# Four modulation pieces, and the first two, as float32 products in two column groups

## The chip, the cores and the metric

The kernel runs on one core of a Trainium2 chip. The metric is the device time of one launch in microseconds (us), as the median of several runs. Traces come from one profiled execution.

## The reference

Two transformer blocks run behind each other on 512 latent rows of width 1024, the first of them with two layers and with 256 context rows beside the latent ones. Everything is float32. What the change touches is in the first block:

```python
for l in range(DEPTH):                      # DEPTH = 2
    last = l == DEPTH - 1
    mod = silu_c @ w_ada[l] + b_ada[l]      # w_ada[l]: 1024 x 6144, six pieces of 1024 columns
    sh1, sc1, gt1, sh2, sc2, gt2 = [m[:, None, :] for m in jnp.split(mod, 6, axis=-1)]
    modc = silu_cc @ w_ada[l] + b_ada[l]
    shc1, scc1, gtc1, shc2, scc2, gtc2 = jnp.split(modc, 6)
    hc = modulate(rmsnorm(xc, g_mix[l]), shc1, scc1)
    pc = hc @ (w_in[l][:, :KV_END] if last else w_in[l])
    ctx_kv = kv_heads(pc[..., :KV_END], kg_a[l], kg_b[l], None)
    h = modulate(rmsnorm(x, g_mix[l]), sh1, sc1)
    p = h @ w_in[l]
    x = x + gt1 * latent_mixer(p, ctx_kv, ...)
    h2 = modulate(rmsnorm(x, g_ffn[l]), sh2, sc2)
    x = x + gt2 * expert_choice_ffn(h2, w_router[l], w_e_gate[l], w_e_up[l], w_e_down[l])
    if not last:
        xc = xc + gtc1 * context_mixer(pc, ctx_kv, ...)
        hc2 = modulate(rmsnorm(xc, g_ffn[l]), shc2, scc2)
        xc = xc + gtc2 * expert_choice_ffn(hc2, w_router[l], w_e_gate[l], w_e_up[l], w_e_down[l])
```

A mixer projects, attends (two kinds of attention and a short convolution), gates the branches (`w_branch`) and ends in the product with `w_out`. The expert stage sends each of 16 experts its best rows by a router. The conditioning has only two rows, `silu_c` and `silu_cc`, so a modulation piece is a product of two rows with 1024 x 1024 weights (4 MB).

## The kernel before

**Order of the stages.** Loading and the first two modulation pieces (0 to about 60 us in the trace), latent mixer of layer 0 (to about 662), context mixer of layer 0 (to 917), experts of layer 0 over latent and context rows together (949 to 1530), latent mixer of layer 1 (to 2180), the last expert stage (`last_experts`, 2222 to about 2670), then the second block.

**Dense products.** Weights come in chunks of 512 KB through `weights`: SP issues the load into `raw` (L92), ScalarE rounds it to `wh` (L95), VectorE subtracts to `wl` (L96), and TensorE runs three matmuls of the reduced float32 format for each pair of operands (L82 to L84). The pools in `self.wps` take turns; `nraw` and `nw` are the number of `raw` buffers and of `wh` and `wl` buffers. The context mixer has two pools, one of 3 and 3 and one of 2 and 2 (`w1`). The expert stages load chunks of 1 MB as `eraw`; the one of layer 0 splits them (`eh` on ScalarE, `el` on VectorE), `last_experts` multiplies them as plain float32 (L1273).

**Modulation.** `ada(l, pieces)` is a generator that the mixers step in the background, one step each `period` ticks. A step is a quarter of a piece: two chunks by `weights`, 16 matmuls with `wh` (L441) and `wl` (L442), a copy on ScalarE, two transposes (L447). In layer l's latent mixer the pieces 2 to 5 of that layer run so, in the context mixer the pieces 0 and 1 of layer 1. The pieces 0 and 1 of layer 0 run ahead of everything in `first_ada`: 64 matmuls of 256 columns in plain float32 (L478) on 16 loads `wada` of 512 KB (L475). `first_gather` runs one small indirect load on GpSimd in the first mixer.

**The end of a mixer.** The product with `w_out` hands each of 8 feature rows to `residual`, which loads `xo` (L928, SP), forms `xn` (L929, VectorE), then `put` forms `u` on ScalarE and the router's matmuls (L970). `finish` sums the norm (L979), forms the affinities `aff`, runs top-k, and transposes `u` (`hpt`, L1002) into token rows `tok`, which GpSimd stores to `h2d` (L1015); the rows are gathered for the experts by an indirect load on GpSimd (L1140, in the last stage L1280) and transposed (`ept`, L1132).

**What sets the order.** The code is recorded and a scheduler orders the instructions of each engine ahead of time. An engine runs its list in order: a load on SP that waits for its buffer holds all the loads behind it.

## Time and profile before

| | us |
|---|---|
| median of 3 runs | 3576.55 (3576.17 to 3577.59) |
| the profiled execution | 3583.02 |
| its span in the trace | 3581.3 |
| TensorE busy | 3354.1 (94%) |
| TensorE weight loads | 2572.3 (72%) |
| VectorE busy | 2268.4 (63%) |
| ScalarE busy | 1732.4 (48%) |
| GpSimd busy | 274.4 (8%) |
| mean granted TensorE clock | 0.977 |

PE is TensorE's matmuls, DVE VectorE, ACT ScalarE, POOL GpSimd, SP the engine that issues most loads. Busy time is a union of instruction spans; a plain float32 matmul leaves two records. "PEclk" is the granted TensorE clock as a share of full speed. A chain of waits shows "[idle before <-releaser]" behind an instruction that its engine sat idle for.

### The profile page before, as it was taken

The numbers are of one execution on the slowest core, as the hardware profiler recorded it, in microseconds if no ns is written. First come the engines' busy times: TensorE is split into PE (matmuls) and PEld (weight loads), VectorE is DVE, ScalarE is ACT, GpSimd is POOL, SyncE is SP. The second block draws the span as 40 slices with busy tenths as digits, with TensorE's granted clock in tenths as the row PEclk, the third lists the DMA queues.
The fourth block names the chain that finished last, engine by engine and source line by source line (L and its number), as shares of the span: only waits on it lengthen the run. The fifth ranks groups of instructions, "written<-read, shape, count | busy, mean of one in ns | idle before, by whom it ended". The sixth has DMA issues, their size and how long they took to land. (4 is left out here: it accounts for less than half of the span.)

```text
span 3581.3 us, 46471 instructions
## 1 busy us (share of the span) xinstructions
PE 3354.1 (94%) x17762; PEld 2572.3 (72%) x17762; DVE 2268.4 (63%) x3543; ACT 1732.4 (48%) x2542; POOL 274.4 (8%) x322
## 2 busy tenths in 40 slices
PE   8999999999799999989999996998889999989998
PEld 5787777898688888877777774332228887768887
DVE  4787676588599999977776753232235456854444
ACT  3555554456477777745555542110115355633333
POOL 1101110000200000021011101000001000010000
PEclk9999999999899999989999997999999999999999
DMA  6332437458799999933334376999993432244332
GB/s 218 119 100 93 135 122 220 145 168 239 269 373 335 367 339 341 350 127 95 100 101 130 121 235 255 421 421 421 421 367 103 128 87 88 84 130 138 100 94 83
DMA packets 369227, 732.90 MB, mean 205 GB/s; under 512 B 25534, under 2 KB 262060, under 8 KB 342636
## 3 DMA queue, kind: packets, MB, share of 16 engines
q1 hardware_dynamic: 355728, 695.15, 55.1%
q0 software_dynamic: 7184, 33.31, 2.4%
q8 instruction: 140, 2.29, 0.3%
q10 hardware_dynamic: 6092, 1.47, 0.2%
q14 instruction: 83, 0.68, 0.1%
HBM read 683.71 MB, written 46.14 MB: 204 GB/s over the span
## 5 line engine op out<-in xcount | busy, mean ns | idle before, releaser
L96 DVE TENSOR_TENSOR wl<-raw,wh 128x1024 fp32r<-128x1024 f32 (+2 forms) x423 | 506.6, 1200 | 370.6 <-ACT wh L95 362.9
L95 ACT ACTIVATE wh<-raw 128x1024 fp32r<-128x1024 f32 (+2 forms) x423 | 436.6, 1034 | 490.4 <-PE d L83 301.0
L82 PE MATMUL d<-hh,wh 128*128 128x512 f32 (+1 forms) x1304 | 485.4, 373 | 5.5 <-ACT hh L301 4.3
L83 PE MATMUL d<-hl,wh 128*128 128x512 f32 (+1 forms) x1304 | 484.1, 371 | 1.8 <-DVE hl L302 1.6
L84 PE MATMUL d<-hh,wl 128*128 128x512 f32 (+1 forms) x1304 | 484.3, 372 | 0.4 <-DVE wl L96 0.4
L1116 DVE TENSOR_TENSOR el<-eraw,eh 128x2048 fp32r<-128x2048 f32 x192 | 433.8, 2287 | 33.2 <-ACT eh L1115 32.5
L1115 ACT ACTIVATE eh<-eraw 128x2048 fp32r<-128x2048 f32 x192 | 365.3, 1918 | 105.6 <-PE pup L84 39.3
L82 PEld LDWEIGHTS d<-hh,wh 128*128 128x128 f32 x1304 | 247.6, 190 | 44.1 <-ACT hh L301 5.1
L83 PEld LDWEIGHTS d<-hl,wh 128*128 128x128 f32 x1304 | 247.3, 190 | 39.8 <-DVE hl L302 4.6
L84 PEld LDWEIGHTS d<-hh,wl 128*128 128x128 f32 x1304 | 247.3, 190 | 39.2 <-DVE wl L96 2.3
L642 ACT ACTIVATE prob<-S,st 128x768 f32<-128x768 f32 (+3 forms) x176 | 134.5, 764 | 142.2 <-DVE st L640 66.9
L1332 DVE SCALAR_TENSOR_TENSOR y<-pdn,route,y 64x512 fp32r<-64x512 f32 x32 | 24.0, 750 | 280.6 <-ACT y L1331 280.5
L82 PE MATMUL d<-wh,hh 128*128 128x256 f32 (+1 forms) x528 | 161.2, 305 | 1.9 <-ACT hh L301 1.8
L83 PE MATMUL d<-wl,hh 128*128 128x256 f32 (+1 forms) x528 | 159.9, 303 | 0.3 <-DVE wl L96 0.3
L84 PE MATMUL d<-wh,hl 128*128 128x256 f32 (+1 forms) x528 | 159.7, 303 | 0.2 <-DVE hl L302 0.2
L638 DVE TENSOR_REDUCE st<-S 128x1 f32<-128x768 f32 (+3 forms) x176 | 137.2, 783 | 23.5 <-PE S L703 21.3
L658 ACT ACTIVATE pth<-ppt 128x512 fp32r<-128x512 f32 x184 | 106.0, 595 | 74.8 <-PE ppt L655 71.5
L659 DVE TENSOR_TENSOR ptl<-ppt,pth 128x512 fp32r<-128x512 f32 x184 | 122.6, 685 | 27.2 <-ACT pth L658 26.1
L1273 PE MATMUL pdn<-eraw,at 128*64 128x512 f32 x512 | 119.0, 599 | 21.1 <-DMA eraw<-in_w_e_down 16.4
L655 PE MATMUL ppt<-ident,prob 128*128 128x128 f32 x736 | 121.6, 277 | 7.2 <-DVE prob L647 6.6
L1273 PE MATMUL pup<-eraw,xt 128*64 128x512 f32 x512 | 119.9, 600 | 6.0 <-DMA eraw<-in_w_e_up 6.0
L1273 PE MATMUL pga<-eraw,xt 128*64 128x512 f32 x512 | 118.5, 605 | 2.7 <-DMA eraw<-in_w_e_gate 2.7
(546 smaller groups left out, 7596.4 us busy)
## 6 DMA issues: line engine op xcount, KB each, us to landing
eraw<-in_w_e_gate SPq DMA_DIRECT2D x128, 1024.0 KB
eraw<-in_w_e_up SPq DMA_DIRECT2D x128, 1024.0 KB
eraw<-in_w_e_down SPq DMA_DIRECT2D x128, 1024.0 KB
raw<-in_w_in SPq DMA_DIRECT2D x170, 512.0 KB
raw<-in_w_ada SPq DMA_DIRECT2D x80, 512.0 KB
raw<-in_w_ff SPq DMA_DIRECT2D x64, 512.0 KB
raw<-in_w_out SPq DMA_DIRECT2D x32, 512.0 KB
raw<-in_w_branch SPq DMA_DIRECT2D x48, 256.0 KB
```

Of the source, the lines that this page charges most:

```text
L82: mm(ps, wh, xh, start=first, stop=False, skip_group_check=skip)
L83: mm(ps, wh, xl, start=False, stop=False, skip_group_check=skip)
L84: mm(ps, wl, xh, start=False, stop=last, skip_group_check=skip)
L95: for ins in (nc.scalar.activation(h[:, :n], raw[:, :n], AF.Copy), nc.vector.tensor_sub(l[:, :n], raw[:, :n], h[:, :n])):
L96: nc.vector.tensor_sub(l[:, :n], raw[:, :n], h[:, :n])):
L638: nc.vector.tensor_reduce(nm, S[:, s0:s1], axis=AX, op=ALU.max, negate=True)
L642: nc.scalar.activation(p, S[:, s0:s1], AF.Exp, bias=nm, accum_out=ls)
L655: nc.tensor.transpose(pt[:, h * 128:h * 128 + 128], probs[h], self.ident)
L659: nc.vector.tensor_sub(pl, pt, ph)
L1115: nc.scalar.activation(h, raw, AF.Copy)
L1116: nc.vector.tensor_sub(lo, raw, h)
L1273: nc.tensor.matmul(ps[halves[j], :], x(k), raw[:, i, j * 512:j * 512 + 512], start=k == 0, stop=k == 7, skip_group_check=True)
```

## The change

Six edits, all in the first block:

1. `ada_between` (new) forms a piece as plain float32 products without splits: for each of 8 slices of 128 rows two matmuls of 512 columns, one into PSUM partitions 0 and 1, one into 64 and 65 (two column groups), then two copies on ScalarE, eight transposes, and `modulation` (new). The mixer calls `between()` behind the `w_out` product and ahead of `finish()`. In the context mixer it forms (0, 5), (1, 0) and (1, 1), the pairs being (layer, piece), with 24 chunk loads `zraw` of 512 KB in 5 buffers of a new pool `z`; in layer 1's latent mixer it forms (1, 5) with four `zraw` of 1 MB in the two `qT` buffers of attention. These four leave the background.
2. `first_ada` runs the pieces 1 and 0 side by side in the two column groups, on the same loads.
3. The context mixer's second weight pool goes: 3 `raw` and 3 `w` buffers in place of 5 and 5.
4. The background in the latent mixers has three pieces and a period of 4 in place of four and 3.
5. `finish` takes its small sum from pool `pd` (now called `nps`) in place of an attention bank.
6. `first_gather` goes; the context residual's store goes from GpSimd's queue to ScalarE's.

```diff
     def first_ada(self, raw):
...
         for q in range(4):
-            for p in (1, 0):
-                ps = self.pd.tile([128, 512], F32, name="d", tag="d")[:2, :256]
-                c0 = p * 1024 + q * 256
-                for ch in range(0, 8, 4):
+            ps = self.pd.tile([128, 512], F32, name="d", tag="d")[:, :256]
+            for ch in range(0, 8, 4):
+                ws = []
+                for p in (1, 0):
                     w = raw[:, n % 4].rearrange("p (k f) -> p k f", k=4)
                     n += 1
+                    c0 = p * 1024 + q * 256
...
-                    for k in range(4):
-                        nc.tensor.matmul(ps, self.cs[:, ch + k, :], w[:, k], start=ch + k == 0, stop=ch + k == 7)
+                    ws.append(w)
+                for k in range(4):
+                    for h, w in zip((0, 64), ws):
+                        nc.tensor.matmul(ps[h:h + 2], self.cs[:, ch + k, :], w[:, k], start=ch + k == 0,
+                                         stop=ch + k == 7, skip_group_check=True)
...
-    def first_gather(self):
...
+    def ada_between(self, l, p, raw, banks, row):
...
+        nc = self.nc
+        ps, pt = banks()
+        k = 0
+        while k < 8:
+            w = raw()
+            n = w.shape[1]
+            nc.sync.dma_start(w, self.A["w_ada"][l][k * 128:(k + n) * 128, p * 1024:p * 1024 + 1024]
+                              .rearrange("(i p) f -> p i f", p=128))
+            for i in range(n):
                 for j in range(2):
+                    nc.tensor.matmul(ps[64 * j:64 * j + 2], self.cs[:, k, :], w[:, i, j * 512:j * 512 + 512],
+                                     start=k == 0, stop=k == 7, skip_group_check=True)
+                k += 1
+        for j in range(2):
+            rows = row()
+            nc.scalar.activation(rows[:2], ps[64 * j:64 * j + 2], AF.Copy)
+            for m in range(4):
+                n = (j * 4 + m) * 2
+                nc.tensor.transpose(pt[:, n:n + 2], rows[:2, m * 128:m * 128 + 128], self.ident[:2, :2])
+        self.modulation(l, p, pt[:, :16], 0, 8)
...
         self.do(self.fm(self.A["w_out"][l], 8, 0, 1024, mh, ml, T, residual))
+        between()
         finish()
...
         def finish():
-            if lat:
-                ps = self.ps.tile([128, 1024], F32, name="S", tag="S")
-            else:
-                ps = self.ps.tile([128, 512], F32, name="S", tag="Sc", bufs=2)
+            ps = self.pd.tile([128, 512], F32, name="nps", tag="d")
...
-                    self.background, self.ticks, self.period = [self.ada(l, (2, 3, 4, 5))], -6, 3
-                    if first:
-                        self.background.append(self.first_gather())
...
+                    self.background, self.ticks, self.period = [self.ada(l, (2, 3, 4))], -6, 4
+
+                    def between():
+                        if first:
+                            return
+                        S = self.ps.tile([128, 1024], F32, name="S", tag="S")
+                        self.ada_between(l, 5, lambda: self.ap.tile([128, 4, TL], F32R, name="zraw", tag="qT", bufs=2)
+                                         .rearrange("p (i a) t -> p i (a t)", i=2).bitcast(F32),
+                                         lambda: [S[:, :512], S[:, 512:]],
+                                         lambda: self.pp.tile([128, 512], F32R, name="zrow", tag="pth").bitcast(F32))
...
-                        more = self.pool(e1, "w1"), 2, 2
+                        zp = self.pool(e1, "z", 5, side="right")
                         self.open_dense(e1, nraw=3, nw=3, side="right")
-                        self.wps.append(more)
+
+                        def between():
+                            for m, p in ((0, 5), (1, 0), (1, 1)):
+                                self.ada_between(m, p, lambda: zp.tile([128, 1, 1024], F32, name="zraw", tag="zraw"),
+                                                 lambda: [self.ps.tile([128, 512], F32, name="S", tag="Sc", bufs=2)
+                                                          for _ in range(2)],
+                                                 lambda: zp.tile([128, 512], F32, name="zrow", tag="zrow", bufs=2))
...
-                        self.background = [self.top_k(True, fp), vectors(), self.load_vectors_2(), self.ada(1, (0, 1))]
+                        self.background = [self.top_k(True, fp), vectors(), self.load_vectors_2()]
...
-                        nc.gpsimd.dma_start(xCd, xC)
+                        nc.scalar.dma_start(xCd, xC)
```

The lists of instructions show three places where the order moves. Buffer numbers stand behind the names; lines of the changed kernel lie 25 to 27 further down (L1002 is L1027 there, L970 is L998, L928 is L955, L1269 is L1294), and L518 is the float32 product of a piece.

TensorE at the end of layer 0's latent mixer, before: `hpt` are the transposes of its `finish`, `d_6501` is the first product of the context mixer.

```order
L84 MATMUL d_6266<-mh_5774,wl_6300 128x512
L1002 MATMUL hpt_6370<-ident_117,u_5975 128x128 x4
L1002 MATMUL hpt_6376<-ident_117,u_5975 128x128 x3
L82 MATMUL d_6501<-wh_6491,hh_6482 128x256
L83 MATMUL d_6501<-wl_6492,hh_6482 128x256
L84 MATMUL d_6501<-wh_6491,hl_6483 128x256
```

And in the changed kernel, where that first product is `d_6340`:

```order
L998 MATMUL o_5853<-wr_5815,u_5814 128x16 x4
L1004 MATMUL nps_6188<-ones_125,acc_5852 128x1 x4
L1027 MATMUL hpt_6215<-ident_117,u_5814 128x128
L1027 MATMUL hpt_6223<-ident_117,u_5814 128x128 x4
L1027 MATMUL hpt_6229<-ident_117,u_5814 128x128 x4
L1027 MATMUL hpt_6237<-ident_117,u_5814 128x128 x4
L1027 MATMUL hpt_6243<-ident_117,u_5814 128x128 x4
L1027 MATMUL hpt_6251<-ident_117,u_5814 128x128 x4
L1027 MATMUL hpt_6257<-ident_117,u_5814 128x128 x4
L82 MATMUL d_6340<-wh_6330,hh_6321 128x256
L83 MATMUL d_6340<-wl_6331,hh_6321 128x256
```

The context mixer's first product, which stood behind seven of the 32 transposes, now stands behind all of them.

TensorE at the end of the context mixer, before, from the last matmuls of `w_out` (`d_9782`) on; `o` is the router's sum, `S` the norm's:

```order
L83 MATMUL d_9782<-ml_9225,wh_9815 128x256
L84 MATMUL d_9782<-mh_9224,wl_9816 128x256
L1002 MATMUL hpt_9913<-ident_117,u_9503 128x128 x4
L1002 MATMUL hpt_9920<-ident_117,u_9503 128x128 x2
L970 MATMUL o_9542<-wr_9504,u_9503 128x16 x2
L1002 MATMUL hpt_9920<-ident_117,u_9503 128x128
L970 MATMUL o_9542<-wr_9504,u_9503 128x16 x2
L979 MATMUL S_9861<-ones_125,acc_9541 128x1 x2
L1002 MATMUL hpt_9920<-ident_117,u_9503 128x128
```

And in the changed kernel, where the last `w_out` product is `d_9327` and the norm's sum `nps_9549` comes six rows behind the last one shown:

```order
L84 MATMUL d_9327<-mh_8847,wl_9361 128x256
L518 MATMUL S_9406<-zraw_9424,cs_147 2x512 x2
L518 MATMUL S_9406<-zraw_9428,cs_147 2x512
L998 MATMUL o_9087<-wr_9049,u_9048 128x16 x2
L518 MATMUL S_9406<-zraw_9428,cs_147 2x512
L518 MATMUL S_9406<-zraw_9432,cs_147 2x512 x2
L518 MATMUL S_9406<-zraw_9436,cs_147 2x512 x2
L1027 MATMUL hpt_9601<-ident_117,u_9048 128x128 x4
L1027 MATMUL hpt_9608<-ident_117,u_9048 128x128 x2
L526 MATMUL S_9407<-ident_117,zrow_9440 128x2 x4
L526 MATMUL S_9407<-ident_117,zrow_9446 128x2 x4
L518 MATMUL S_9453<-zraw_9455,cs_147 2x512 x2
```

The float32 products of the pieces stand between the last `w_out` matmul and the last router matmuls.

SP at the end of layer 1's latent mixer, before: `raw` are chunks of `w_out`, `xo` residual loads, `eraw` the chunks of the last expert stage.

```order
L1269 DMA eraw_20812<-in_w_e_up 128x2048
L928 DMA xo_20385<-xLd_67 128x512
L92 DMA raw_20505<-in_w_out 128x4x256
L1269 DMA eraw_20818<-in_w_e_up 128x2048
L92 DMA raw_20535<-in_w_out 128x4x256
L928 DMA xo_20408<-xLd_67 128x512
L1269 DMA eraw_20824<-in_w_e_up 128x2048
L1269 DMA eraw_20830<-in_w_e_up 128x2048
L928 DMA xo_20469<-xLd_67 128x512
L928 DMA xo_20492<-xLd_67 128x512
L928 DMA xo_20553<-xLd_67 128x512
L928 DMA xo_20576<-xLd_67 128x512
```

And in the changed kernel:

```order
L955 DMA xo_20012<-xLd_67 128x512
L955 DMA xo_20035<-xLd_67 128x512
L955 DMA xo_20096<-xLd_67 128x512
L955 DMA xo_20119<-xLd_67 128x512
L514 DMA zraw_20143<-in_w_ada 128x2x1024
L514 DMA zraw_20149<-in_w_ada 128x2x1024
L1294 DMA eraw_20419<-in_w_e_gate 128x2048
L1294 DMA eraw_20366<-in_w_e_gate 128x2048
L1294 DMA eraw_20372<-in_w_e_gate 128x2048
L1294 DMA eraw_20378<-in_w_e_gate 128x2048
L1294 DMA eraw_20384<-in_w_e_gate 128x2048
```

The eight expert chunks that stood between the `w_out` chunks and the residual loads (two of them earlier, among the branch chunks) now stand behind all residual loads and behind two chunks of the modulation piece.

## Rows read from the trace of the kernel before

**Rows 1.** Windows of several stretches; columns as the first line names them.

```profile
core 0: us, PE busy (x) PEld busy (x) DVE busy (x) ACT busy (x) POOL busy (x), PEclk, DMA share, GB/s
150.00:300.00 150.00, 148.47 (x853) 120.01 (x851) 122.26 (x207) 93.19 (x167) 9.43 (x13) 1.00 0.31 98
700.00:900.00 200.00, 193.16 (x1550) 182.54 (x1549) 166.66 (x383) 126.45 (x238) 11.16 (x10) 1.00 0.68 203
2240.00:2640.00 400.00, 361.70 (x1586) 120.74 (x1582) 111.26 (x168) 43.99 (x71) 4.69 (x5) 1.00 1.01 421
45.00:55.00 10.00, 9.83 (x66) 7.16 (x66) 4.79 (x11) 2.11 (x4) 0.00 (x0) 1.00 1.04 332
2120.00:2140.00 20.00, 17.80 (x82) 14.47 (x80) 12.76 (x22) 7.52 (x11) 0.00 (x0) 0.91 0.87 291
665.00:670.00 5.00, 4.39 (x39) 4.22 (x39) 2.37 (x10) 1.47 (x2) 1.02 (x1) 1.00 0.07 22
900.00:917.00 17.00, 17.00 (x143) 16.86 (x143) 6.72 (x12) 5.02 (x12) 0.00 (x0) 1.00 0.90 342
2184.00:2200.00 16.00, 6.75 (x30) 5.17 (x30) 12.25 (x47) 5.31 (x9) 13.34 (x13) 0.51 0.56 211
2220.00:2230.00 10.00, 9.72 (x38) 4.13 (x40) 0.00 (x0) 1.19 (x2) 0.93 (x1) 0.73 0.83 290
```

**Rows 2.** Timeline of TensorE, ends of layer 0's mixers: start, length, instruction, idle before.

```profile
675.54 0.60 PE L1002 MATMUL hpt<-ident,u 128*128 128x128 f32 x4
...
917.30 0.28 PE L84 MATMUL d<-mh,wl 128*128 128x256 f32 x1
...
920.55 0.58 PE L979 MATMUL S<-ones,acc 128*128 128x1 f32 x4
...
947.76 1.97 PE L1132 MATMUL ept<-ident,xs 128*128 128x128 f32 x8 [17.11 <-DMA xs<-h2d,gidx]
```

**Rows 3.** Timeline of TensorE, one background burst.

```profile
129.04 0.28 PE L441 MATMUL d<-wh,cst 128*4 128x256 f32 x1
...
130.79 0.28 PE L442 MATMUL d<-wl,cst 128*4 128x256 f32 x1
...
131.53 0.28 PE L447 MATMUL apt<-ident,arow 4*128 4x4 f32 x2 [0.23 <-ACT arow L444]
```

**Rows 4.** Groups by form: busy us and mean ns, then idle before them.

```profile
L96 DVE TENSOR_TENSOR wl<-raw,wh 128x1024 fp32r<-128x1024 f32 x386 | 473.9, 1231 | 328.7 <-ACT wh L95 321.2 <-DMA mCd<-gt 3.2 <-PE d L84 1.8
...
L95 ACT ACTIVATE wh<-raw 128x1024 fp32r<-128x1024 f32 x386 | 407.5, 1058 | 446.0 <-PE d L83 292.5 <-issue 43.3 <-DMA raw<-in_w_in 25.3
```

**Rows 5.** Timeline of TensorE, float32 products: first pieces, then the last expert.

```profile
53.99 4.48 PE L478 MATMUL d<-wada,cs 128*2 128x256 f32 x20
...
58.61 2.75 PE L478 MATMUL d<-wada,cs 128*2 128x256 f32 x12
...
2665.48 7.26 PE L1273 MATMUL pdn<-eraw,at 128*64 128x512 f32 x32 [0.75 <-ACT at L1296]
```

**Rows 6.** DMA issues from 655 to 680 us: count, KB each, median us to landing.

```profile
h2d<-tok POOLq DMA_DIRECT2D x4, 512.0 KB, 4.8
```

**Rows 7.** Timeline of SP's queue, ends of the context mixer and of layer 1's.

```profile
910.97 0.33 SPq L928 DMA_DIRECT2D xo<-xCd  x1
...
2085.70 0.35 SPq L1269 DMA_DIRECT2D eraw<-in_w_e_gate  x1
...
2150.98 0.90 SPq L1269 DMA_DIRECT2D eraw<-in_w_e_up  x2
```

**Rows 8.** Timeline of VectorE, end of the context mixer.

```profile
918.65 0.48 DVE L929 SCALAR_TENSOR_TENSOR xn<-d,gt,xo 128x256 f32<-128x256 f32 x1 [1.46 <-DMA xo<-xCd]
...
933.28 6.69 DVE L1116 TENSOR_TENSOR el<-eraw,eh 128x2048 fp32r<-128x2048 f32 x3
```

**Rows 9.** Timeline of GpSimd: the dummy gather, the first gather of each expert stage.

```profile
101.59 1.10 POOL L498 DMA_INDIRECT dummy<-k_ident,zero  x1 [5.10 <-PE rps L251]
...
933.66 7.22 POOL L1140 DMA_INDIRECT xs<-h2d,gidx  x1 [3.97 <-DVE gidx L1092]
...
2211.11 1.03 POOL L1280 DMA_INDIRECT xs<-h2d,gpair  x1 [11.03 <-DMA eraw<-in_w_e_down]
```

More of the change, by code (lines that the diff above doesn't have):

```diff
@@ new lines, in first_ada @@
+            rows = self.tp.tile([128, 512], F32, name="arows", tag="hn", bufs=4)
+            pt = self.pt.tile([128, 512], F32, name="apt", tag="t")
+            for h, p in ((0, 1), (64, 0)):
+                nc.scalar.activation(rows[:2, p * 256:p * 256 + 256], ps[h:h + 2], AF.Copy)
+                for j in range(p * 2, p * 2 + 2):
+                    nc.tensor.transpose(pt[:, j * 2:j * 2 + 2], rows[:2, j * 128:j * 128 + 128], self.ident[:2, :2])
+                self.modulation(0, p, pt[:, p * 4:p * 4 + 4], q * 2, 2)
@@ new lines, in first_ada, with modulation @@
+            yield
+    def modulation(self, l, p, ps, j0, n):
+        nc = self.nc
+        vec, mod = self.vec[l], self.mod[l]
+        c = slice(p * 8 + j0, p * 8 + j0 + n)
+        b = lambda a: a[:, None, :].to_broadcast([128, 2, n])
+        nc.vector.tensor_add(mod[:, :, c], ps.rearrange("p (j i) -> p i j", i=2), b(vec[:, c]))
+        if p in (1, 4):
+            g = (48 if p == 1 else 56) + j0
+            nc.vector.tensor_scalar(mod[:, :, c], mod[:, :, c], 1.0, None, ALU.add)
+            nc.vector.tensor_mul(mod[:, :, c], mod[:, :, c], b(vec[:, g:g + n]))
```

25 lines of the change are left out of this document (4 added, 21 removed).

## The prediction

> **What bounds the kernel now.** I read the busy time by stretch first. In the first layer's latent mixer TensorE works 148.47 of 150 us, in the context mixer 193.16 of 200 us [rows 1]: PE work taken out there comes off the time. From 2240 to 2640 us, in the last expert stage, TensorE works only 361.70 of 400 us, while the DMA share is 1.01 at 421 GB/s [rows 1]: that stage ends when its weight stream ends. Two stretches belong to neither. After the context mixer the last w_out matmul starts at 917.30 and the expert inputs' first transpose at 947.76, of which TensorE sat 17.11 us waiting for gathered rows [rows 2]. After layer 1's mixer a like wait runs from about 2184 to 2222. So the change is costed by place: what it takes from packed mixers, what it puts into waits, and what it does to the queue that feeds the last stage.
>
> **What it takes away.** A background piece is four bursts of 16 matmuls. The first of a burst starts at 129.04, the last at 130.79, so they come every 0.117 us, 1.87 us a burst; the two transposes behind add 0.21 us (131.53 to 131.74) [rows 3]. One piece is 4 x 2.08 = 8.3 us of TensorE, four are 33.3 us: two from the context mixer, one from each latent mixer. The ends: 27 us, if a fifth of the freed slots stays empty because chunks come at their own pace; 37 us, if the lighter VectorE (32 splits of 1.231 us go [rows 4]; it is busy 166.66 of 200 us [rows 1]) closes half of the 6.8 idle us of the context mixer. I take 33.3.
>
> As float32 products in two column groups a piece is 16 matmuls of 512 columns. The last expert stage has the same form: 32 records in 7.26 us [rows 5]. A matmul leaves two records, so this is 0.45 us a matmul, 0.9 a pair, 7.3 us a piece. The 256-column matmuls of the first pieces stand in one group: 32 records from 53.99 to about 61.3, 0.46 us a matmul [rows 5]; 512 columns there would be 0.9, so a pair costs what one alone would. A piece is thus hardly cheaper than its 8.3 us in the background. The gain must come from putting it into waits.
>
> The Trainium skill ("TensorE: Matmul & The Clock Gate", Measured speedup vs the span model) measures 2.38x for three column tiles, about 1.6 for two if that scales; by it (an estimate) a pair would be 1.1 us and the nine or so pairs beside other work would cost 2 us more. The row above has the kernel's own form, and I go by the row.
>
> First two pieces: their 128 records halve, but until 55 us the loads run at a share of 1.04 [rows 1], and faster matmuls only wait for them. What counts is the last burst, 7.3 us, which halves: 3.6 us. Ends 0 and 8 (the burst before it too).
>
> Layer 1's mixer loses 8 early expert loads of 1 MB (below). From 2120 to 2140, while they ran, TensorE missed 2.2 us [rows 1]; I give 1 us back, ends 0 and 2.
>
> Gains: 33.3 + 3.6 + 1 = 37.9 us.
>
> **Latent to context mixer, layer 0.** Before, context chunks had been loaded and split while the latent product ran, and the first context product stands between the transposes of the latent `finish`; TensorE works 4.39 of 5 us there [rows 1]. In the new order all `hpt` transposes stand ahead of the first context product, because the z pool takes the place where the early chunks lay, and the first raw chunk now waits for the last transpose. That transpose depends on token tiles whose stores take 4.8 us [rows 6], so it keeps its time, 675.54 [rows 2]. Then a chunk must land (3 to 5 us; the nearest row is the 512 KB store) and be split on ScalarE (1.058 us [rows 4]). First product at about 681 instead of 663. Between 662.6 and 681 the finish holds some 7 us of TensorE work, so 11.5 us are lost where 1 was: **10.5 us**. Ends 6 (the chunk lands in 2 us and the clock holds) and 14 (the clock falls to 0.51, as after 2184 [rows 1], and returns late).
>
> **Context mixer with 3 and 3 buffers** for 5 and 5. A chunk takes about 2.8 us of TensorE (24 matmuls at 0.117 [rows 3]); three raw buffers turn in some 4 us of loading and 2.3 us of splits, 2.1 us a chunk. It fits, thinly: **3 us**, ends 0 and 10.
>
> **End of the context mixer.** Four and a half pairs stand inside w_out: 4 us. The other nineteen and a half stand in and behind the wait. Two go on the path: three pairs stand between the first expert matmuls (2.7 us). The last residual load `xo` now stands on SP's queue behind two chunk loads that wait for float32 products placed after the last w_out matmul. Before, it was issued at 910.97 and the residual ran at 918.65, 1 us after the product [rows 2, 7, 8]; now it is issued at about 920, behind some 3 MB in flight at 342 GB/s [rows 1], so the residual and everything after it (the norm's sum, 920.55 [rows 2], top-k, gather) come later by 8 us, ends 0 and 11. What was next, the float32 products, fits beside top-k on VectorE and beside the gather.
>
> The gather: 7.22 us on GpSimd, while three `el` subtractions ran on VectorE from 933.28 for 6.69 us; the same kind of gather in layer 1, with VectorE idle, took 1.03 [rows 8, 9]. In the new order two, not three, stand there: 2.2 us back, ends 0 and 4. The Trainium skill ("SBUF — State Buffer", SBUF: two separate sides) says that a VectorE operation with two SBUF inputs holds the port pair that it shares with GpSimd. By that rule the gather gets shorter, and the trace agrees in its 7.22 beside 6.69.
>
> Sum here: 4 + 2.7 + 8 - 2.2 = **12.5 us**, from 4 to 20.
>
> **The last expert stage.** Before, 8 loads of 1 MB went out between 2085.70 and 2152, hidden in the mixer [rows 7]. In the new order all of them stand on SP behind two 1 MB chunk loads whose buffers come free only when float32 products after the last w_out matmul have run. The stream, the bound of this stage, thus starts at about 2184 and has 10 MB more to carry: 10.49 MB at 421 GB/s is 24.9 us. Idle that it can fill: 16 us at 211 GB/s of 421 (8 us) and 10 us at 290 (3 us) [rows 1]. Left: **14 us**, ends 9 (the first loads overtake) and 25 (nothing is filled). The piece itself lies in the wait.
>
> The dummy gather took 1.10 us beside other work [rows 9]: nothing.
>
> **The sum.** Losses 10.5 + 3 + 12.5 + 14 = 40.0; gains 37.9. The profiled execution, 3583.0 us, goes to 3585.1. It stood 6.5 us above the median of 3576.55, so I forecast 3578.6, call it **3579 us**: no change that can be told (0.2%, 7 us, is what a measurement of this kernel can tell).
>
> **Rivals.**
> *Faster.* The chain behind the context mixer is not delayed: the `xo` loads land as early as before. For it: several residual loads are issued before the waiting chunks; against: the last is not. That gives back the 8 us, and a lighter VectorE the 3.4 us beside it: 3579 - 11 = 3568.
> *Slower: the stream isn't filled.* Its fifth load waits for a chunk whose products stand behind the finish's transposes. If that falls after the first four have landed (later than about 2199: six MB from 2184 at 2.5 us), the idle time of 2184 to 2230 stays and the stage pays 25 us instead of 14: 3590. Against it: those products stand behind transposes that ended early in the wait.
> *Slower: thin buffers.* Three raw chunks don't carry the context mixer; it pays 10 us, not 3: 3586. The DMA share there is 0.68 [rows 1], which leaves room, but SP issues in order.
> *The gather stays long.* It was long because it was the first, not because of `el`: the 2.2 us don't come, and without the dummy it may grow by another such 6.2 us (7.22 - 1.03 [rows 9]): 3581 to 3587. The Trainium skill ("GPSIMD Engine Reference", Instruction dispatch) has a first call of freshly loaded code pay about 6 us. Against it: the dummy's 1.10 us showed no such thing, and the first real one was still long.
> *The column groups don't run side by side here.* A pair is 1.8 us: w_out and the expert product pay 7 us more, the first pieces gain nothing: 3590. The 32 records in 7.26 us [rows 5] speak against it.
>
> **Chances.** Forecast 0.40, faster rival 0.27, unfilled stream 0.14, thin buffers 0.09, long gather 0.05, column groups 0.05. Faster by over 0.2%: the faster rival and a little of the forecast's spread, 0.29. Slower: stream and groups whole, buffers and gather in most, a little of the forecast, 0.29. Within: 0.42. The forecast's own bounds, with the terms' ends taken as independent, are some 12 us either way; to hold 8 in 10 with the rivals I take 3562 to 3596.
>
> **What would show it.** Right: the latent `finish` followed by a TensorE gap of some 5 us before the first context product, near 680 less what the mixer gained; the last context residual 8 us later after its product; a gather of about 5 us; the weight stream of the last stage unbroken from the last w_out product, and that stage longer by about 14 us from that product to its end; each mixer shorter by 8 to 16 us. Wrong: the last stage no longer than before, because its loads went out earlier than SP's order says; a gap at the context's start under 2 us; or mixers that keep their length, with new waits of TensorE for splits.

## The result

The changed kernel takes 3606.06 us (median of 4 runs, 3603.48 to 3608.02), the kernel before, timed beside it, 3576.36 us. The ratio is 1.0082, 95% interval 1.0069 to 1.0094: slower by 30 us, above the range of 3562 to 3596 and 27 us above the forecast. The profiled execution of after took 3603.48 us, its span is 3601.7 us.

**By place.** The starts of the last products of the stages, read from the timelines of TensorE in both traces, cut the span into six pieces. The last column is what the sum of the prediction gave for the same piece.

| stretch | before, us | after, us | measured | predicted |
|---|---|---|---|---|
| start to the last w_out product, latent mixer of layer 0 | 661.95 | 654.97 | -7.0 | -11.9 |
| from there to the last w_out product of the context mixer | 255.35 | 256.91 | +1.6 | +0.9 |
| from there to the last expert product of layer 0 | 628.04 | 641.73 | +13.7 | +8.5 |
| from there to the last w_out product, layer 1 | 634.48 | 632.70 | -1.8 | -9.3 |
| from there to the last product of the last expert stage | 492.32 | 508.63 | +16.3 | +14 |
| the second block | 909.11 | 906.77 | -2.3 | 0 |
| sum | 3581.25 | 3601.71 | +20.5 | +2.2 |

The span grew by 20.5 us, the sum had 2.2. Two latent mixers that gained 8.8 us instead of 21.2 are 12.4 of these 18.3 us, and the end of the context mixer, with 5.2, is the next. The second row comes out right by two errors that cancel, as the runs below show.

**Windows of after** (to be held against [rows 1]):

```profile
core 0: us, PE busy (x) PEld busy (x) DVE busy (x) ACT busy (x) POOL busy (x), PEclk, DMA share, GB/s
655.00:658.00 3.00, 1.13 (x10) 0.81 (x8) 1.86 (x5) 1.24 (x2) 0.00 (x0) 1.00 0.00 0
664.00:667.00 3.00, 3.00 (x15) 2.47 (x13) 2.19 (x7) 0.26 (x1) 1.07 (x2) 0.50 0.42 175
...
676.00:682.50 6.50, 5.81 (x25) 5.51 (x26) 3.67 (x3) 2.11 (x2) 0.00 (x0) 0.50 0.93 318
682.50:690.00 7.50, 7.50 (x63) 7.50 (x62) 3.82 (x5) 3.15 (x5) 0.57 (x1) 0.98 0.50 154
...
2220.00:2230.00 10.00, 0.00 (x0) 0.00 (x0) 0.88 (x2) 0.00 (x0) 2.00 (x2) 0.50 1.01 426
2240.00:2640.00 400.00, 355.99 (x1554) 118.15 (x1552) 103.89 (x157) 43.94 (x70) 4.69 (x5) 1.00 1.01 421
```

The last stage is still bound by its stream (421 GB/s, share 1.01). TensorE now rests in 2220 to 2230, where it worked 9.72 of 10 us before, and the stream runs there at 426 GB/s instead of 290: the bytes that were loaded early before are loaded now. At 676 the context mixer starts at a granted clock of 0.50 (the level of 1.2 GHz) and is back at 2.4 GHz from about 682.5 on. The clock had fallen long before: at about 659 us, behind a stretch in which TensorE worked 1.13 of 3 us. In the kernel before, where context products stood among the transposes, it was 1.00 from 655 to 680 us.

**Latent to context mixer**, timeline of TensorE (start, length, instruction, idle before; against the first of [rows 2]):

```profile
668.33 1.97 PE L1027 MATMUL hpt<-ident,u 128*128 128x128 f32 x8 [0.91 <-DVE tok L1031]
676.01 0.58 PE L82 MATMUL d<-wh,hh 128*128 128x256 f32 x1 [5.71 <-ACT wh L95]
```

The first context product starts 21.0 us behind the last w_out product (654.97). The idle 5.71 us are the gap foretold. The transposes ahead of it already run at half clock, and so do the 6.5 us of products behind it.

**End of the context mixer**, timelines of VectorE, TensorE, GpSimd and SP (against [rows 2, 7 to 9]):

```profile
918.91 0.17 DVE L498 TENSOR_TENSOR mod<-S,vec 128x16 f32<-128x16 f32 x1 [8.75 <-PE S L526]
919.00 0.48 DVE L956 SCALAR_TENSOR_TENSOR xn<-d,gt,xo 128x256 f32<-128x256 f32 x1
...
921.99 0.48 DVE L956 SCALAR_TENSOR_TENSOR xn<-d,gt,xo 128x256 f32<-128x256 f32 x1 [1.55 <-DMA xo<-xCd]
...
938.12 4.49 DVE L1141 TENSOR_TENSOR el<-eraw,eh 128x2048 fp32r<-128x2048 f32 x2 [1.17 <-DMA h2d<-tok]
```

```profile
923.89 0.58 PE L1004 MATMUL nps<-ones,acc 128*128 128x1 f32 x4
...
950.48 1.51 PE L1157 MATMUL ept<-ident,xs 128*128 128x128 f32 x6 [8.71 <-DMA xs<-h2d,gidx]
```

```profile
930.15 0.60 POOL L1040 DMA_DIRECT2D h2d<-tok  x1 [0.30 <-POOL tok L1034]
...
933.57 0.57 POOL L1040 DMA_DIRECT2D h2d<-tok  x1 [0.30 <-POOL tok L1034]
941.67 1.87 POOL L1165 DMA_INDIRECT xs<-h2d,gidx  x1 [7.53 <-DMA zraw<-in_w_ada]
```

```profile
915.92 0.38 SPq L955 DMA_DIRECT2D xo<-xCd  x1
916.39 23.27 SPq L514 DMA_DIRECT2D zraw<-in_w_ada  x13
```

The last residual load goes out at 915.92 instead of 910.97, the norm's sum starts 12.0 us behind the last w_out product (911.88) instead of 3.25 us. The gather takes 1.87 us instead of 7.22, but starts only 8.1 us after the last token store was issued at 933.57; the trace puts that wait down to the chunk loads that were then in flight. The lists of transfers (count, KB each, median us from issue to landing) show that the stores themselves landed late. Before:

```profile
h2d<-tok POOLq DMA_DIRECT2D x2, 512.0 KB, 2.9
```

And in the changed kernel:

```profile
h2d<-tok POOLq DMA_DIRECT2D x2, 512.0 KB, 7.2
```

The residual had a second cause of delay: VectorE's list puts the first piece's `mod` ahead of the last two residuals, and VectorE waited 8.75 us there for that piece's transposes (L526). The last residual then waited another 1.55 us for its load.

**Start of the last stage**, SP's queue of after: two chunk loads of the piece, then all expert chunks.

```profile
2188.56 4.03 SPq L514 DMA_DIRECT2D zraw<-in_w_ada  x2
2192.64 7.96 SPq L1294 DMA_DIRECT2D eraw<-in_w_e_gate  x5
```

### The profile page after: what moved, and what is told of

Read it like the earlier page. It is cut to its first block, busy times and chain, and to the rows that moved or that the text cites. A ratio compares the mean times of both kernels' runs of the same rounds, so it can differ in the third digit from the quotient of the medians.

```text
span 3601.7 us, 46078 instructions
## 1 busy us (share of the span) xinstructions
PE 3360.1 (93%) x17625; PEld 2554.1 (71%) x17634; DVE 2234.1 (62%) x3480; ACT 1700.4 (47%) x2502; POOL 272.5 (8%) x320
## 5 line engine op out<-in xcount | busy, mean ns | idle before, releaser
L96 DVE TENSOR_TENSOR wl<-raw,wh 128x1024 fp32r<-128x1024 f32 (+2 forms) x391 | 466.2, 1195 | 386.0 <-ACT wh L95 375.7
L95 ACT ACTIVATE wh<-raw 128x1024 fp32r<-128x1024 f32 (+2 forms) x391 | 403.3, 1032 | 507.8 <-PE d L83 316.7
```

The costliest lines, as they stand in the source:

```text
L95: for ins in (nc.scalar.activation(h[:, :n], raw[:, :n], AF.Copy), nc.vector.tensor_sub(l[:, :n], raw[:, :n], h[:, :n])):
L96: nc.vector.tensor_sub(l[:, :n], raw[:, :n], h[:, :n])):
```

## The experiments

Three edits looked costly in the traces: the z pool that pushes the early context chunks out, the piece in layer 1, and the new period. Each was undone in a run of its own; the second of these runs also puts layer 1's period back to 3. Edits 5 and 6 stand in all runs but that of the first pieces alone, and no run tests either of them by itself.

### The weight pools opened ahead of the z pool

```diff
-                        zp = self.pool(e1, "z", 5, side="right")
                         self.open_dense(e1, nraw=3, nw=3, side="right")
+                        zp = self.pool(e1, "z", 5, side="right")
```

> The changed kernel with one edit: in layer 0's context mixer the dense pools are opened ahead of the z pool, so that the early context chunks have their old place and the z buffers take the place that waits. Theory (the place of the z pool holds the context's start): the first context product again stands among the last transposes of the latent mixer; the stretch from the last latent w_out matmul to the context's first product, 21.0 us in the changed kernel, falls to about 1 us, and the time falls by 14 us (10 to 18). Rival (the transition is long because only 3 raw buffers are left, w1 being gone): the gap stays over 10 us, the time falls by under 5 us.

Measured 3586.52 us, 1.0024 (1.0014 to 1.0034): 19.5 us less than the changed kernel. From the latent mixer's last w_out product to the context mixer's it takes 240.74 us instead of 256.91. TensorE in this kernel:

```profile
660.22 0.46 PE L1027 MATMUL hpt<-ident,u 128*128 128x128 f32 x1
660.61 0.58 PE L82 MATMUL d<-wh,hh 128*128 128x256 f32 x1
...
663.78 0.60 PE L1027 MATMUL hpt<-ident,u 128*128 128x128 f32 x4
664.14 0.36 PE L82 MATMUL d<-wh,hh 128*128 128x256 f32 x1
```

The first product stands among the transposes again and starts at 660.61, 5.3 us behind the last w_out product (about 1 us was expected), and the gap is gone. Held against the same dense products of the kernel before, the changed kernel goes from 7.0 us ahead to 9.3 us behind across the transition (16.3 lost), this one from 6.6 to 5.5 us ahead (1.1 lost). The order of two pool openings, which decides on whose old memory the first chunks land, was worth 15 us there. The other 4 us come off layer 0's experts (595.5 us from first to last product, 599.5 in the changed kernel), between whose first products no pairs stand in this order.

### Layer 1's piece back in the background

```diff
-                    self.background, self.ticks, self.period = [self.ada(l, (2, 3, 4))], -6, 4
+                    self.background, self.ticks, self.period = [self.ada(l, (2, 3, 4) if first else (2, 3, 4, 5))], -6, 4 if first else 3
-                    xL = self.mixer(l, True, hl, xLd, mLd, gLd, kvc, sink, self.xlp, h2d, 0, xL, arrive(), between)
+                    xL = self.mixer(l, True, hl, xLd, mLd, gLd, kvc, sink, self.xlp, h2d, 0, xL, arrive())
```

> The changed kernel with piece 5 of layer 1 back in the background of its latent mixer (four pieces, period 3 there), nothing between w_out and finish there; the rest as changed. Theory (the last expert stage is bound by its weight stream, which the piece's chunk loads hold back): the stretch from layer 1's last w_out matmul to the last product of the last experts, 508.6 us in the changed kernel and 492.3 before, falls back by 15 us (12 to 18); layer 1's mixer, whose length the piece shortened by only 1.8 us, gets longer by about 2 us; together 13 us less. Rival (that stage is longer because its gather and first products start later by 6 us): it falls by 6 us or less.

Measured 3596.08 us, 1.0047 (1.0029 to 1.0064), 10 us less than the changed kernel. Expert chunks go out between the w_out chunks again, and the last stage takes 493.7 us, 508.6 in the changed kernel, 492.3 before:

```profile
2155.85 0.38 SPq L92 DMA_DIRECT2D raw<-in_w_out  x1
2156.28 0.50 SPq L1294 DMA_DIRECT2D eraw<-in_w_e_up  x1
```

So 15 of the 16 us of that stage hang on the eight loads that the piece holds back. Layer 1's mixer, which has the piece again and period 3, takes 637.7 us instead of 632.7. A piece in layer 1's wait costs more than the same piece in the background.

### Period 3

```diff
-                    self.background, self.ticks, self.period = [self.ada(l, (2, 3, 4))], -6, 4
+                    self.background, self.ticks, self.period = [self.ada(l, (2, 3, 4))], -6, 3
```

> The changed kernel with the background's period 3 in place of 4 in both latent mixers, three pieces as changed. Theory (at period 4 the first quarter piece falls where its splits and transposes stall TensorE, the gaps at 134.66, 139.61 and 154.39 in the changed kernel's trace, some 5 us in each mixer): both latent mixers get shorter by 5 us each, the time falls by 10 us (5 to 14). Rival (a mixer that is so full gives back part of any freed matmuls as idle time, wherever they stood): under 3 us.

Measured 3593.76 us, 1.0042 (1.0029 to 1.0056), 12.3 us less than the changed kernel with the same work. Layer 0's last w_out product starts at 649.77 instead of 654.97, layer 1's mixer takes 625.24 us instead of 632.70. One place where the time goes: the waits of TensorE from 130 to 160 us in the changed kernel,

```profile
135.69 0.28 PE L441 MATMUL d<-wh,cst 128*4 128x256 f32 x1 [1.03 <-ACT wh L95]
136.57 0.69 PE L723 MATMUL S<-kT,qT 128*128 128x512 f32 x1 [0.60 <-ACT prob L669]
140.67 0.28 PE L447 MATMUL apt<-ident,arow 4*128 4x4 f32 x2 [1.06 <-ACT arow L444]
157.48 1.23 PE L652 MATMUL qpt<-identr,qhl 128*128 128x128 f32 x8 [3.09 <-DVE qhl L646]
```

and the window 130 to 160 us, first in the changed kernel, then with period 3:

```profile
130.00:160.00 30.00, 24.22 (x149) 20.26 (x149) 21.62 (x36) 15.74 (x26) 10.71 (x9) 0.90 0.27 86
```

```profile
130.00:160.00 30.00, 28.69 (x187) 23.36 (x187) 25.04 (x39) 19.60 (x33) 8.83 (x9) 1.00 0.28 86
```

With period 4 the first burst of the background (L441 to L447) falls into attention, where its splits share ScalarE and VectorE with the heads' work; TensorE works 24.2 of 30 us at a clock of 0.90. With period 3 it works 28.7 at 1.00, as before (28.78). The same four waits stand in layer 1 from 1664 to 1687 us. The run shows what the period costs; that the splits' share of the two engines is the reason is read from these waits and was not tested apart.

### The residual loads on ScalarE's queue

```diff
-            nc.sync.dma_start(xo, x_dram[:, j, :])
+            (nc.sync if lat else nc.scalar).dma_start(xo, x_dram[:, j, :])
```

> The changed kernel with the context mixer's eight residual loads xo issued on ScalarE's queue instead of SP's, where chunk loads of the pieces stand ahead of the last ones. Theory (the last residual load stands behind chunk loads that wait for products): the last residual comes 1 us after its product instead of 10 us (921.99 less 911.88), everything behind it earlier by 6 to 9 us, the first expert product too; the time falls by 6 us. Rival (the stores of the token rows and the gather are held by the chunk loads on the DMA engines, whenever they begin): the norm's sum comes earlier but the first expert product by under 3 us.

Measured 3611.47 us, 1.0091 (1.0073 to 1.0109), 5 us more than the changed kernel: a miss. No chunk load holds the last `xo` here, and the last residual runs 5.8 us behind the last w_out product (912.84) instead of 10.1. Yet the norm's sum starts at 924.37, 11.5 us behind that product (12.0 in the changed kernel). Timelines of ScalarE's queue, VectorE and ScalarE:

```profile
914.09 0.36 ACTq L955 DMA_DIRECT2D xo<-xCd  x1
```

```profile
918.60 0.48 DVE L956 SCALAR_TENSOR_TENSOR xn<-d,gt,xo 128x256 f32<-128x256 f32 x1 [3.65 <-DMA xo<-xCd]
```

```profile
922.56 0.59 ACT L523 ACTIVATE zrow<-S 2x512 f32<-2x512 f32 x1 [7.66 <-PE S L518]
...
923.06 0.40 ACT L993 ACTIVATE sq<-xn 128x256 f32<-128x256 f32 x1
```

The load was issued 1.25 us behind the last w_out product, because ScalarE's list puts it behind the squares of the row before, and it landed some 4.5 us later. Then ScalarE, which forms the squares (`sq`) for the sum, sat 7.66 us in front of the piece's copy `zrow`, which stands ahead of the last squares and waits for the piece's products. With the load out of the way, the order of the piece's instructions on ScalarE holds the sum. The last token store was issued at 935.25, the gather ran from 943.55, and the first expert product comes 47.5 us behind the last w_out product (42.2 in the changed kernel), which is the 5 us.

### The first two pieces alone

The kernel before with the change of `first_ada` only: one tile for both pieces, and

```diff
+                for k in range(4):
+                    for h, w in zip((0, 64), ws):
+                        nc.tensor.matmul(ps[h:h + 2], self.cs[:, ch + k, :], w[:, k], start=ch + k == 0,
+                                         stop=ch + k == 7, skip_group_check=True)
```

> The kernel before with one part of the change: the first two pieces side by side in the two column groups, nothing else. Theory (only the last burst, behind the last load, counts): the latent mixer of layer 0 begins and ends 2 to 4 us earlier, the time falls by 3 us (1 to 5). Rival (the front is bound by its loads to the end): under 1 us.

Measured 3575.05 us, 0.9992 (0.9983 to 1.0001). The interval just holds no change; in the trace layer 0's last w_out product starts 3.9 us earlier than before (658.07), near the 3.6 us of the prediction.

### The three edits undone together

The changed kernel with the weight pools first, layer 1's piece in the background and period 3.

> The changed kernel with the three edits that each gave time: dense pools opened ahead of the z pool, piece 5 of layer 1 back in the background, period 3 in both latent mixers. Theory (three separate losses at three places): they add up, -19 -10 -12, so about 3565 us, 13 us under the kernel before; the last expert stage as before (492 us from the last w_out product), the context mixer's start as before, the end of the context mixer still 17 us dearer. Rival (some of the three are one loss seen twice): over 3575.

Measured 3566.60 us, 0.9963 (0.9949 to 0.9976). The three single gains add up to 41.8 us, together they give 39.5. That fits three separate causes, but not in every part. The run with layer 1's piece back already had period 3 there, so the 7.5 us that layer 1 gave in the run of the period cannot come a second time: its mixer takes 637.8 us here, as it did there. Each single gain is known only to some 6 us either way, by the intervals of the two ratios that it is the difference of, so the sum cannot tell. What is left of the change, three pieces at the end of the context mixer, the shorter latent mixer and the first pieces, beats the kernel before by 12 us.

### Residual loads ahead of the w_out product

As the last one, with the eight `xo` of the context mixer loaded into buffers of their own in the z pool ahead of w_out:

```diff
+        early = []
+        if xop is not None:
+            for j in range(8):
+                early.append(xop.tile([128, T], F32, name="xo", tag="xo", bufs=8))
+                nc.sync.dma_start(early[j], x_dram[:, j, :])
```

> As the run with three edits undone, and the context mixer's eight residual loads go to buffers of their own (8 KB a partition in the z pool) and are issued ahead of its w_out product, so that neither SP's order nor the chunk loads in flight hold them. Theory (the end of the context mixer is late because its last residual waits for its load): the norm's sum comes about 4 us after the last w_out matmul, as before, instead of 12, and the first expert product 7 us earlier: 3558. Rival (the stores of token rows and the gather land late behind the chunk loads and take the wait's place): the norm's sum is early, but the first expert product gains under 3 us.

Measured 3563.22 us, 0.9952 (0.9938 to 0.9965): 3.4 us less than the last one. VectorE now forms the last residual 0.3 us behind the last w_out product (885.69), but TensorE's list still has five pairs of the piece ahead of the norm's sum:

```profile
886.00 0.48 DVE L965 SCALAR_TENSOR_TENSOR xn<-d,gt,xo 128x256 f32<-128x256 f32 x1
```

```profile
893.88 0.61 PE L1013 MATMUL nps<-ones,acc 128*128 128x1 f32 x4
```

From the last w_out product to the first expert product it takes 41.4 us, as in the run before it (41.1). Of the 3 us the traces give 1.1 to the context mixer, out of whose w_out product the pairs have gone, and 1.9 to layer 0's latent mixer, whose code is the same in both. The rival's time came, and here too the wait already ends with the last chunk of the pieces, not with the gather:

```profile
922.64 1.03 PE L518 MATMUL S<-zraw,cs 128*2 128x512 f32 x4 [0.25 <-DMA zraw<-in_w_ada]
...
925.37 1.92 PE L1166 MATMUL ept<-ident,xs 128*128 128x128 f32 x8
```

### `finish` ahead of the pieces

```diff
-        between()
+        if lat:
+            between()
         finish()
+        if not lat:
+            between()
```

> The kernel of e7_and_xo_loaded_early, with the context mixer's finish recorded ahead of its three float32 pieces, so that two pairs of L518 instead of five stand between the last w_out product and the norm's sum. Theory (the order of TensorE's list held the sum 8.2 us behind the last w_out product): the sum starts 4 to 5 us behind it, the expert inputs' first product 36 to 39 us behind it instead of 41.4; 3559 to 3561. Rival (the token stores, which land 8 us after their issue behind the pieces' loads, set the gather): the sum comes early, the first expert product stays 40 to 42 us behind; 3562 to 3564.

Measured 3561.58 us, 0.9947 (0.9934 to 0.9961). The sum starts 3.0 us behind the last w_out product (889.17), as early as before the change, and the first expert product still comes 40.6 us behind. That is the rival's time, but not by its mechanism:

```profile
919.18 1.03 PE L518 MATMUL S<-zraw,cs 128*2 128x512 f32 x4 [1.48 <-DMA zraw<-in_w_ada]
920.60 1.03 PE L518 MATMUL S<-zraw,cs 128*2 128x512 f32 x4 [0.39 <-DMA zraw<-in_w_ada]
921.88 1.03 PE L518 MATMUL S<-zraw,cs 128*2 128x512 f32 x4 [0.25 <-DMA zraw<-in_w_ada]
...
928.43 1.09 PE L1169 MATMUL ept<-ident,xs 128*128 128x128 f32 x8
```

```profile
910.02 2.18 POOL L1177 DMA_INDIRECT xs<-h2d,gidx  x1 [7.54 <-DVE el L1153]
923.19 0.97 POOL L1177 DMA_INDIRECT xs<-h2d,gidx  x1 [10.99 <-PE S L518]
```

The products stand ahead of `ept` on TensorE and wait for one chunk after the other, 1.28 us apart; `ept` (no idle before it) follows the last transposes of the piece. The second gather, too, is put down to such a product. The wait ends with the stream of the pieces' own loads: from 907 to 928 us the DMA share is 1.00 at 389 GB/s.

### One piece at the end, two in the background

```diff
-                            for m, p in ((0, 5), (1, 0), (1, 1)):
+                            for m, p in ((0, 5), ):
-                        self.background = [self.top_k(True, fp), vectors(), self.load_vectors_2()]
+                        self.background = [self.top_k(True, fp), vectors(), self.load_vectors_2(), self.ada(1, (0, 1))]
```

> The kernel of e8_finish_ahead_of_pieces with the pieces (1, 0) and (1, 1) back in the context mixer's background, so only (0, 5) is formed at its end, on three loads behind the last w_out product instead of some twenty. Theory (at the end of the context mixer the three pieces' loads and products cost about 9 us and the mixer gives back 16.6): from the last w_out product to the expert inputs' first product 32 to 34 us, as in the kernel before; token stores land 3 to 4 us after issue; the context mixer 15 to 17 us longer than in e8; 3566 to 3570. Rival (with three weight buffers the mixer can't carry the splits of the background too): context mixer over 20 us longer; above 3572.

Measured 3577.87 us, 0.9999 (0.9990 to 1.0008). From the last w_out product (923.70) to the first expert product it takes only 22.9 us, ten less than the theory said and nine less than before the change: the residual comes early, and the gather starts 4.1 us behind the last token store (issued 936.19, gather 940.25), where it took 8.1 in the run above. The stores land 2.9 us after their issue here, 7.3 in the run above, and the gather waits only for its index. The context mixer takes 36.3 us more than in the run above, more than the rival's 20:

```profile
870.00:875.00 5.00, 1.46 (x10) 0.59 (x8) 1.23 (x1) 1.73 (x2) 0.00 (x0) 1.00 1.13 231
875.00:880.00 5.00, 4.82 (x27) 4.29 (x25) 1.97 (x4) 0.73 (x2) 0.00 (x0) 0.66 0.72 159
```

```profile
873.03 0.28 PE L441 MATMUL d<-wh,cst 128*4 128x256 f32 x1 [2.56 <-ACT wh L95]
874.29 0.28 PE L442 MATMUL d<-wl,cst 128*4 128x256 f32 x1 [0.98 <-DVE wl L96]
...
887.73 0.28 PE L441 MATMUL d<-wh,cst 128*4 128x256 f32 x1 [1.29 <-ACT wh L95]
```

About 17 us are the two pieces and 4.5 us the float32 pairs that stand in the mixer at 866 us; some 9 us more are waits, most of them for splits (idle of 13.6 us from 700 us on, against 4.7 in the run above and 6.1 in the kernel before, which has the same two pieces and five buffers), and some of the rest the clock. So three weight buffers carry the mixer, as long as no background piece takes chunks from them; that the buffers, and not the float32 pairs in the middle, make these waits was not run apart.

### Two pieces at the end

The run with `finish` ahead, and the piece (0, 5) back in layer 0's latent mixer:

```diff
-                    [self.ada(l, (2, 3, 4) if first else (2, 3, 4, 5))], -6, 3
+                    [self.ada(l, (2, 3, 4, 5))], -6, 3
-                            for m, p in ((0, 5), (1, 0), (1, 1)):
+                            for m, p in ((1, 0), (1, 1)):
```

> The kernel of e8_finish_ahead_of_pieces with the piece (0, 5) back in the background of layer 0's latent mixer (four pieces there, period 3), so 16 instead of 24 chunk loads at the end of the context mixer. Theory (in e8 the wait ends with the stream of these loads: the last 18 came at 1.28 us each on a DMA share of 1.00, and the gathered rows had long landed): eight chunks fewer take 8 x 1.28 = 10 us off that end, until the chain of top-k, token store and gather binds, which took 23 us without such loads and some 8 us more with them; from the last w_out product to the first expert product 31 to 34 us instead of 40.6; layer 0's latent mixer 7 to 9 us longer; the kernel within 3 us of e8. Rival (the chain, not the stream, sets that wait): it keeps 39 to 41 us, and the kernel is slower than e8 by the piece's 7 to 9 us, 3568 to 3571.

Measured 3560.54 us, 0.9933 (0.9920 to 0.9946). The wait is 32.0 us (898.38 to 930.37), 8.6 us less than with three pieces, and the latent mixer ends 8.0 us later: the stream theory holds. Now TensorE waits for gathered rows again:

```profile
928.60 1.94 PE L1169 MATMUL ept<-ident,xs 128*128 128x128 f32 x8 [3.99 <-DMA xs<-h2d,gidx]
```

The third piece costs at the end about what it costs in the background: 3561.58 and 3560.54 us. Single traces can't tell more, for stretches with the same work differ between them by several us (layer 1's mixer, whose code is the same in both, takes 636.8 us in the trace with three pieces and 631.5 in the one with two). The last three kernels with three or two pieces there lie between 3560.5 and 3563.2 us, and all beat both kernels.

## Why the prediction was wrong

**Price of a piece, 8.3 us: right, as far as the traces tell.** Two pieces out of the context mixer were forecast at 16.6 us and gave some 17 to 20 in the traces. Layer 0's last w_out product stands at 646.4 to 650.3 us in the five traces with three background pieces at period 3, and at 658.1 and 658.3 in the two with four and the new first pieces: 8 to 12 us for one.

**Period 4: the step that was missing.** The diff lists it as edit 4, and the prediction gave it no cost. It took 12.3 us by the medians; in the traces 5.2 us of layer 0 and 7.5 of layer 1 come back with period 3. The step that failed is "One piece is 4 x 2.08 = 8.3 us of TensorE, four are 33.3 us": it held for the work and left out that the bursts which stay were moved, onto heads where TensorE waits for ScalarE and VectorE. A wait for ScalarE inside a burst was in the profile (the 0.23 us of [rows 3]), at the old place; the new place was readable only in the order of the instructions. With period 3 alone the changed kernel measured 3593.76 us, near the upper end of the stated range of 3562 to 3596.

**Latent to context mixer: right mechanism, too small.** Forecast 10.5, measured 16.3 against the kernel before, and 15 of them came back when the pools changed places. The first product came at 676.01, some 2 us behind what was said ("about 681 instead of 663", less the 7.0 us that the mixer gained). The rest of what was mis-sized is behind it: 6.5 us at half clock, by which some 3 us are lost, and a first split that leaves the next matmul waiting 0.68 us. The upper end of 14 named the clock, from the wait after 2184 [rows 1]. It should have been the value taken: with the context's products gone from among the transposes, TensorE had too little to do in `finish`, and the clock fell at 659 us, 11 us ahead of the gap.

**Three weight buffers: 3 us forecast, none seen.** With the weight pools first, the lead of the context mixer's products against the kernel before stays the same to half a us from 700 to 800 us, until the pieces come off. This and the term above cancel in part, which is why the second row of the table looks right. The rival of thin buffers falls for this kernel; the run with background pieces shows where it would have decided.

**End of the context mixer: 8.5 us net of the pairs in w_out, measured 13.7.** The residual was right in time: the sum came 8.8 us later behind the last w_out product (8 forecast). Its load was held as foretold; that VectorE and ScalarE, too, meet a piece's instructions ahead of the last residuals was not in the forecast. The gather did shorten, from 7.22 to 1.87 us, and nothing came back. Its start moved: the token store was issued 933.57 and the gather could run at 941.67, about 8 us on; in the kernel before the second store went out at 929.14, and the gather at 933.66 waited only for its index (3.97 <-DVE gidx L1092). The stores landed 7.2 us after their issue instead of 2.9. The step "In the new order two, not three, stand there: 2.2 us back" took the gather's length for the path and did not ask what is late next: its start, behind chunk loads that filled 0.97 of the DMA time from 912 to 950 us. The pairs cost 3.8 us between the experts (2.7) and some 4 in w_out (4).

**The last stage: right.** 16.3 us against 14, stream unbroken from the issue at 2192.64 on (354 GB/s up to 2200, 409 and more behind it), and the run with the loads back in the mixer returns it. The rival of an unfilled stream asked for 25 us.

**From profile to median: 9 us of the miss.** The forecast took the profiled execution as 6.5 us above the median. The median of the kernel before lay at 3578.5 to 3581.4 us in the later comparisons, so part of that was chance; the profiled execution of after lies 2.6 us below its median.

**The rivals.** The faster one needed `xo` to land early; moving it to another queue brought the residual 4.3 us forward and the sum 0.5, and loading it early brought the residual to 0.3 us behind its product, for no gain in that wait until `finish` and the chunk loads were changed too. The long gather fell: without the dummy, the first gather took 1.87 us, or 1.05 where it began 0.3 us ahead of the first `el`. The column groups run side by side: in the changed kernel 12 records, three pairs, take 2.74 us behind 924.58, 0.91 a pair, as forecast.

## What to carry to other kernels

Work that is moved into a wait brings its loads with it: price the bytes against the wait's own stores and gathers, whose landing time (here 2.9 us without and some 7 us with chunk loads in flight) sits on the path. The work itself also brings its place in the list of every engine: a copy or an addition of the new piece that stands ahead of the old chain holds it, whichever queue loads the data. A pool opened in another order, or a period of a background loop, is an edit like any other, and each was worth more here than a modulation piece; ask of every buffer whose memory it inherits, and of every moved burst which splits it meets. When a wait is shortened at one end, look for the stream that ends it at the other before the gain is booked.

## What the runs showed of the hardware

**A gather on GpSimd and subtractions on VectorE.** In the run with one piece at the end, the first gather began 0.3 us ahead of the `el` subtractions, the second ran beside them:

```profile
940.25 1.05 POOL L1177 DMA_INDIRECT xs<-h2d,gidx  x1 [3.49 <-DVE gidx L1129]
941.60 4.28 POOL L1177 DMA_INDIRECT xs<-h2d,gidx  x1 [0.30 <-issue]
```

```profile
940.55 4.48 DVE L1153 TENSOR_TENSOR el<-eraw,eh 128x2048 fp32r<-128x2048 f32 x2
```

The long one ended at 945.88, 0.85 us behind the end of the last `el` (945.03). In the kernel before the gather ended 0.91 us behind the last `el`, in the changed kernel 0.93, and in the other runs in which a first gather of layer 0 began during an `el`, 0.9 us behind the end of one of them. The Trainium skill ("SBUF — State Buffer", SBUF: two separate sides) says that a VectorE operation with two SBUF inputs can hold a port pair that it shares with GpSimd; the gathers that began during an `el` agree. The one that began ahead of it kept its 1.05 us, and the two `el` beside it their 4.48. Why the gather sometimes gets through at the end of the `el` that runs (912.20 behind 911.28, in the run with `finish` ahead) and sometimes only after a row of three (7.22 us before) was not settled. The same skill ("GPSIMD Engine Reference", Instruction dispatch) gives the first call of freshly loaded code some 6 us: the 1.05 us above, the first gather in a program without the dummy, show nothing of it.

**Landing behind bulk loads.** Token stores of 512 KB landed 2.9 us after their issue where few loads ran (the kernel before, and one piece at the end, at DMA shares of 0.31 and 0.40), and 7.2 to 7.4 us after it behind chunk loads (changed kernel at a share of 0.97, residual loads on ScalarE's queue, `finish` ahead). In the nine traces with two or three pieces at the end the gather began 7.6 to 8.5 us behind the issue of the last store. A residual load of 128 KB that was issued behind the chunks reached VectorE after some 6 us from SP's queue (issued 915.92, residual at 921.99) and after 4.5 from ScalarE's (914.09 and 918.60).

**The clock in a starved stretch.** In the changed kernel TensorE worked 1.13 of 3 us from 655 to 658, and at about 659 the granted clock fell from 1.00 to 0.50, the level of 1.2 GHz. It stayed there through 3 us of unbroken transposes (664 to 667), the idle 5.71 us and the first 6.5 us of context products, which lost some 3 us by it. In the kernel before, with context products among the same transposes (4.39 of 5 us busy from 665 to 670), it stayed at 1.00.
